# Two build turns per query tile in layer 1, more fill beside the first head, two stores on another queue: a two-layer hybrid block on one core

## The chip, the core and the metric

The kernel runs on one core of a Trainium2 chip. The metric is the device time of one execution in microseconds (us); a time is the median of several executions. TensorE (PE) multiplies matrices into PSUM, VectorE (DVE), ScalarE (ACT) and GpSimd (POOL) work on vectors, and SyncE (SP) issues most transfers. Each engine runs its own instructions in order, and engines wait for one another by semaphores.

## What is computed

Two layers of a block over 1024 tokens and 256 context tokens, width 1024, float32. One projection feeds a gated convolution, a neighbourhood attention (8 heads) and a window attention (8 query heads, 2 key heads); their gated outputs are projected, merged and added to the input. Cut to what matters here:

```
for l in range(2):
    h  = rms_norm(x,   norm_g[l]) * (1 + scale)   + shift
    hc = rms_norm(ctx, norm_g[l]) * (1 + scale_c) + shift_c
    (a_glu, a_gate, nq, nk, nv, n_gate, wq, wk, wv, w_gate, merge) = split(h @ w_in[l])
    o_na = neighbourhood_attention(rms_norm(nq), rms_norm(nk), nv, context keys and values, rpb)
    o_wa = window_attention(rope(rms_norm(wq)), rope(rms_norm(wk)), wv, context ..., sink)
    y = sigmoid(g_a)*conv_branch(...) + sigmoid(g_b)*((o_na*silu(n_gate)) @ w_b) + sigmoid(g_c)*((o_wa*silu(w_gate)) @ w_c)
    x = x + gate * (y @ w_o)
    ctx likewise, in layer 0 only
```

Head size is 64. A query tile is 128 tokens, so a head has 8 query tiles in layer 1 and 10 in layer 0, where the context has queries too.

## The kernel before

A value is kept as a high part rounded to float32r and a low part, the remainder, and products are sums of several matmuls of such parts. In each layer comes first an **attention stage**, then the branches (gates L932, projections L947) and the output pass (L984).

**What sets the order.** PE's instructions run in the order in which the program writes them (L1015, a manual schedule for PE alone). The order on the other engines is chosen at compile time. So whatever PE has to wait for holds up all PE work written behind it.

**The attention stage** (`attention`, L1018) goes through 16 heads, 0 to 7 neighbourhood heads and 8 to 15 window heads. For each query tile it writes: the scores (`sp`, L582 and L584, with the query half `qst` as the loaded weights); some fill; the turn of the probabilities of an earlier tile (`tp`, L614, 4 or 5 transposes, copied by ACT into `pt`, L617, and split by DVE, L618); the softmax weights of this tile; a step of the build of the next head; more fill; and the product with the values of a tile before (`pv`, L625).

**Fill** (class `Fill`) is PE work that needs no attention result: projections of the head groups (`u_ps`, L339), the convolution's inputs (`glu_g`, `glu_v`) and merge gates (`mg_ps`, L714). `pull(ns)` issues pieces until their estimated time reaches `ns`; what is not used in the attention stage comes right after it, where the merge gates run beside the convolution on DVE.

**The build of a head** (`build_head`, L422) loads raw keys and queries, multiplies them by their norms on POOL (`nrm` L439, `nrmq` L465), and turns them in parts: a **turn** is 4 transposes of 128x128 on PE into `t_ps` (L408; 2 for the context keys), then an ACT copy of the high part (`kh` L449, `qst` L472), then a DVE subtraction for the low part (`kl` L450, `qst` L473). The tile `t_ps` comes from a pool of one buffer (`ps_tr`, `bufs=1`), so the transposes of a turn wait until DVE has read the turn before. A neighbourhood head in layer 1 has five turns, three for keys and two for queries. So have the window heads 8 and 12; the other window heads have the two query turns.

The build is a generator. Its first step issues the loads, step k after it normalises part k and turns part k-1, and the last step turns the last part. Tile 0 of the running head takes the first step; from tile 1 on (even heads) or tile 2 on (odd heads) each tile takes one step (L1052). What is left at the head's end runs before the next head. So in layer 1 a five-turn build ends in tile 6 of an even head and in tile 7, the last, of an odd one.

Head 0 has no head before it. Its build runs ahead of the tiles, with a pull of fill after each step (L1034 to L1038), but none after the last turn. The output pass ends with 16 stores of the result, all issued by POOL (L1009).

Of the kernel before, what the change touches and what calls it, by code (L numbers as in the profile page):

```python
# [18 lines left out]
L = 2  # L19
# [21 lines left out]
KC = 8  # L41
# [9 lines left out]
def hybrid_block_kernel(  # L51
# [9 lines left out]
    nc = tc.nc  # L61
# [460 lines left out]
    def wa_build(l, head, st, lc, pb, hs):  # L522
        u, j = 4 + head // 4, head % 4
        yield from build_head(
            l, st, u, pb, j % 2, False, (256, 4) if j == 0 else None, (j * 64, j) if j % 2 == 0 else None, -0.125
        )
        hs.update(kk=st["k"], qt=st["q"])
# [145 lines left out]
    def load_block(src, pw, eng=(nc.gpsimd, nc.gpsimd)):  # L673
        return chunks_of([load_w(src[:, 4 * i:4 * i + 4, :], pw, eng[i]) for i in range(2)])

    def run(gen):
        for _ in gen:
            pass
# [45 lines left out]
    def mm_tile(name):  # L724
        return ps_mm.tile([128, 512], F32, tag="mm", name=name)
# [3 lines left out]
    def s_tile(name):  # L729
        flip[0] ^= 1  # L730
        if flip[0]:
            return ps_s.tile([128, 1024], F32, tag="s", name=name)
        return ps_t.tile([128, 1024], F32, tag="t", name=name)
# [250 lines left out]
    def output_pass(l, gis, y, ysp, pw, xsrc, norms=None, side=iter(())):  # L984

        dst = out if l == L - 1 else x1_d

        def load(f):
            xr = {}
            for gi in gis:  # L990
                o, n = GROUPS[gi]
                xr[gi] = pw.tile([128, 512], F32, tag="t", bufs=3, name="xr")
                nc.sync.dma_start(out=xr[gi][:, 0:n], in_=xsrc[f][:, o:o + n])
            return load_block(wO[l, f], pw, (nc.vector, nc.vector)), xr

        nxt = load(0)
        for f in range(KC):
            w, xr = nxt
            for gi in gis:
                o, n = GROUPS[gi]  # L1000
                ci = 1 if gi == 2 else 0
                ps = s_tile("wo_ps") if (f * len(gis) + gi) % 2 else mm_tile("wo_ps")
                run(product(w, KC, ysp[gi], n, ps))
                if gi == gis[0] and f + 1 < KC:
                    nxt = load(f + 1)
                nc.vector.scalar_tensor_tensor(
                    y[gi][:, f, :], ps[:, 0:n], mods[l][:, 16 + f, ci:ci + 1], xr[gi][:, 0:n], ALU.mult, ALU.add
                )
                nc.gpsimd.dma_start(out=dst[f][:, o:o + n], in_=y[gi][:, f, :])  # L1009
                if norms:  # L1010
                    norms[gi].add(y[gi][:, f, :], f)
            next(side, None)
            next(side, None)
# [4 lines left out]
    def attention(l, st, lc, pb, fill):  # L1018
        need = {0: 0, 2: 1, 4: 2, 6: 3, 8: 4, 12: 5}
        info = [{} for _ in range(16)]  # L1020
        mask_t = pb.tile([128, 896], F32, name="mask_t")
        nc.sync.dma_start(out=mask_t, in_=wa_mask)
        bias_t = [pb.tile([128, 640], F32, name=f"bias{i}") for i in range(2)]
        for bt in bias_t:
            nc.gpsimd.memset(bt[:, 384:640], 0.0)

        def build(i):
            if i in need:
                fill.finish(f"u{need[i]}")
            if i < 8:  # L1030
                return na_build(l, i, st, lc, pb, info[i])
            return wa_build(l, i - 8, st, lc, pb, info[i])

        first = build(0)  # L1034
        next(first)
        fill.pull(FIRST_NS)
        for _ in first:
            fill.pull(1500.0)  # L1038
        last = []
        for i in range(16):  # L1040
            nxt = None
            tiles = na_tiles(l, i, lc, pb, info[i], bias_t, mask_t) if i < 8 else wa_tiles(l, i - 8, st, lc, pb, info[i], mask_t)
            for n, tile_ in enumerate(tiles):
                tile_.scores()
                f = FILL_NS[l] * (0.6 if tile_.w == 0 else 1.0)
                fill.pull(f * 0.5)
                if len(last) > TL - 1:
                    last[-TL].turn()
                tile_.weights()
                if n == 0 and i < 15:  # L1050
                    nxt = build(i + 1)
                if nxt is not None and (n == LOAD_AT or n > BUILD_AT[l][i % 2]):  # L1052
                    next(nxt, None)
                fill.pull(f * 0.5)
                if len(last) > TL:
                    last[-TL - 1].values()
                last = last[-TL:] + [tile_]
            if nxt is not None:
                run(nxt)
        for i in range(TL, 0, -1):  # L1060
            last[-i].turn()
            fill.pull(1800.0)
            last[-i - 1].values()
        fill.pull(1800.0)
        last[-1].values()
        flush()
# [113 lines left out]
    for l in range(L):  # L1180
# [3 lines left out]
        fill = Fill()  # L1184
# [48 lines left out]
        y = {gi: py.tile([128, KC, GROUPS[gi][1]], F32, name=f"y{gi}") for gi in range(ngr)}  # L1233
# [149 lines left out]
```

## Time and profile before

| | us |
|---|---|
| median of three runs | 2761.24 (2760.91 to 2761.47) |
| the profiled execution's own time | 2762.03 |
| its span, first to last instruction | 2759.1 |
| PE busy in the span | 2687.4 (97%) |
| DVE, ACT, POOL busy | 1783.4, 1133.0, 865.9 |

The profile is of one execution; the 2.9 us between its time and its span lie outside the instructions. With one engine busy for 97% of the span, the question for any change is where that engine waits: the rows are read for PE's idle pieces, given in brackets behind the instruction that followed them, with the instruction that ended them. Layer 1's attention stage lies from about 1599 us to 2110 us of the span. The granted clock is the share of TensorE's full speed.

### The profile page before, as it was taken

What the parts mean: (1) busy time and instruction counts of PE and PEld (TensorE: products, weight loads), DVE (VectorE), ACT (ScalarE), POOL (GpSimd) and SP (SyncE); (2) the same over time, 40 slices, a digit from 0 to 9 for tenths busy, and PEclk for the clock granted to TensorE, in tenths of its full rate; (3) what the DMA queues carried; (4) which work ended last, traced back from release to release, by engine and by line L of the source; (5) the groups of instructions that cost most, each with busy time, mean ns of one, the idle gap of its engine ahead of it and who ended that gap; (6) DMA issues with size and microseconds to landing.
All of it is one profiled execution on the core that took longest, in us unless ns stands there. A gap on an engine that the chain in (4) does not pass through costs nothing. (4 is left out here: it accounts for less than half of the span.)

```text
span 2759.1 us, 43655 instructions
## 1 busy us (share of the span) xinstructions
PE 2687.4 (97%) x14996; PEld 2342.2 (85%) x14996; DVE 1783.4 (65%) x3842; ACT 1133.0 (41%) x2500; POOL 865.9 (31%) x1122
## 2 busy tenths in 40 slices
PE   7899999999999999999999999999999999999999
PEld 3899998989888888787888899999888888778887
DVE  4667777766499934778375566766765699372162
ACT  2466666656511113321333356655556322232220
POOL 0044374633400004245501123375424200235610
PEclk9999999999999999999999999999999999999999
DMA  7365444211233332645364355452212243354343
GB/s 253 95 177 151 128 118 117 73 52 35 87 115 115 117 100 73 210 143 177 101 194 157 101 150 155 136 142 86 81 41 78 93 145 111 105 182 139 103 151 105
DMA packets 321293, 337.35 MB, mean 122 GB/s; under 512 B 81840, under 2 KB 240688, under 8 KB 321072
## 3 DMA queue, kind: packets, MB, share of 16 engines
q1 hardware_dynamic: 300848, 296.81, 36.3%
q10 hardware_dynamic: 17280, 28.32, 2.7%
q0 software_dynamic: 2944, 9.44, 0.9%
q8 instruction: 118, 1.93, 0.3%
q14 instruction: 103, 0.84, 0.1%
HBM read 244.02 MB, written 90.44 MB: 121 GB/s over the span
## 5 line engine op out<-in xcount | busy, mean ns | idle before, releaser
L714 PE MATMUL mg_ps<-hh,wf 128*128 128x512 f32 (+1 forms) x1920 | 565.9, 374 | 2.3 <-POOL wf L670 1.3
L339 PE MATMUL u_ps<-wu,hh 128*128 128x384 f32 (+2 forms) x1872 | 485.0, 342 | 9.9 <-DVE vr L371 4.2
L714 PEld LDWEIGHTS mg_ps<-hh,wf 128*128 128x128 f32 x1920 | 347.1, 188 | 69.4 <-POOL wf L670 2.1
L670 POOL TENSOR_TENSOR wf<-rf,wf 128x512 fp32r<-128x512 f32 x118 | 156.6, 1329 | 706.6 <-ACT wf L669 701.0
L714 PE MATMUL mg_ps<-hl,wf 128*128 128x512 f32 (+1 forms) x960 | 356.8, 372 | 0.0
L608 POOL TENSOR_SCALAR p<-p,rd 128x640 f32<-128x640 f32 (+1 forms) x288 | 216.4, 752 | 406.4 <-DVE rd L606 240.5
L339 PEld LDWEIGHTS u_ps<-wu,hh 128*128 128x128 f32 x1872 | 318.8, 190 | 15.4 <-DVE vr L371 4.5
L600 ACT ACTIVATE p<-p,nmx 128x641 f32<-128x641 f32 (+3 forms) x288 | 222.2, 771 | 236.2 <-DVE nmx L596 112.8
L339 PE MATMUL u_ps<-wu,hl 128*128 128x384 f32 (+2 forms) x936 | 312.4, 334 | 0.7 <-DVE hl L274 0.7
L669 ACT ACTIVATE wf<-rf 128x512 fp32r<-128x512 f32 x240 | 150.6, 628 | 342.1 <-PE pp_ps L714 165.5
L714 PE MATMUL pp_ps<-ogh,wf 128*128 128x512 f32 (+1 forms) x960 | 279.6, 373 | 5.0 <-ACT ogh L865 2.4
L714 PE MATMUL gt_ps<-hh,wf 128*128 128x512 f32 (+1 forms) x960 | 284.0, 377 | 0.0
L618 DVE TENSOR_TENSOR pt<-tp,pt 128x640 fp32r<-128x640 f32 (+1 forms) x288 | 215.7, 749 | 98.7 <-ACT pt L617 96.1
L916 ACT ACTIVATE mg_t<-mg_ps 128x512 f32<-128x512 f32 (+1 forms) x120 | 66.6, 555 | 361.2 <-PE mg_ps L714 360.8
L714 PEld LDWEIGHTS pp_ps<-ogh,wf 128*128 128x128 f32 x960 | 174.7, 189 | 42.7 <-ACT ogh L865 3.7
L714 PEld LDWEIGHTS mg_ps<-hl,wf 128*128 128x128 f32 x960 | 180.4, 188 | 33.2
L714 PEld LDWEIGHTS gt_ps<-hh,wf 128*128 128x128 f32 x960 | 174.0, 188 | 36.5 <-issue 1.9
L614 PE MATMUL tp<-ident,p 128*128 128x128 f32 x1280 | 187.4, 273 | 15.6 <-DVE pt L618 7.2
L772 DVE SCALAR_TENSOR_TENSOR cv_out<-cv_in,lc_conv_w,cv_out 128x1024 f32<-128x1024 f32 (+1 forms) x192 | 194.2, 1011 | 0.0
L617 ACT ACTIVATE pt<-tp 128x640 fp32r<-128x640 f32 (+1 forms) x288 | 181.8, 631 | 20.6 <-PE tp L614 19.4
L614 PEld LDWEIGHTS tp<-ident,p 128*128 128x128 f32 x1280 | 153.5, 140 | 43.1 <-POOL p L608 13.8
L714 PE MATMUL wo_ps<-hh,wf 128*128 128x512 f32 (+1 forms) x640 | 184.1, 372 | 0.0
(174 smaller groups left out, 5459.5 us busy)
## 6 DMA issues: line engine op xcount, KB each, us to landing
rf<-in_wF SPq DMA_DIRECT2D x144, 256.0 KB, 2.8
ru<-in_wU SPq DMA_DIRECT2D x104, 192.0 KB, 3.5
bias<-in_na_bias SPq DMA_DIRECT2D x96, 192.0 KB, 2.6
w_ada_s<-in_w_ada SPq DMA_DIRECT2D x64, 256.0 KB, 3.3
nrm<-qk_d SPq DMA_DIRECT2D x40, 320.0 KB, 4.2
rf<-in_wP SPq DMA_DIRECT2D x48, 256.0 KB, 2.7
rf<-in_wO SPq DMA_DIRECT2D x48, 256.0 KB, 3.4
v_d<-vr SPq DMA_DIRECT2D x80, 128.0 KB, 2.0
```

The source lines that it names most:

```text
L339: nc.tensor.matmul(ps[:, c0:UW], lhsT=a[:, k, off * 128:(off + 1) * 128], rhs=w[:, b, c0:UW], start=(k == 0 and i == 0), stop=(k == KC - 1 ...
L600: nc.scalar.activation(self.p[:, 0:n], self.p[:, 0:n], AF.Exp, bias=m, scale=1.0 if sink is None else -1.0, accum_out=self.den)
L608: nc.gpsimd.tensor_scalar(p, p, rd, 1.0, ALU.mult, ALU.mult)
L614: nc.tensor.transpose(tp[:, c * 128:(c + 1) * 128], self.p[:, c * 128:(c + 1) * 128], ident)
L617: nc.scalar.activation(self.pt[:, 0:nch, 0, :], tv, AF.Copy)
L618: nc.vector.tensor_tensor(self.pt[:, 0:nch, 1, :], tv, f32(self.pt[:, 0:nch, 0, :]), ALU.subtract)
L669: nc.scalar.activation(w[:, 0, 0:n, :], raw[:, 0:n, :], AF.Copy)
L670: eng.tensor_tensor(w[:, 1, 0:n, :], raw[:, 0:n, :], f32(w[:, 0, 0:n, :]), ALU.subtract)
L714: nc.tensor.matmul(ps[:, 0:n], lhsT=w(k, b), rhs=a[:, k, 0:n], start=(k == 0 and i == 0), stop=(k == kn - 1 and i == 2),)
L772: nc.vector.scalar_tensor_tensor(r, a[:, k:k + n], tap, r, ALU.mult, ALU.add)
L916: nc.scalar.activation(t[:, 0:n], ps[:, 0:n], AF.Tanh, scale=0.5)
```

## The change

In `attention`, in layer 1 alone, tiles 3 and 5 take a second step of the build. In the build of head 0, in both layers, each pull of fill is of 2300 ns instead of 1500. In the output pass of layer 1 the stores of the last row block (f = 7) are issued by SP instead of POOL; there are two, one for each token group.

```diff
-                nc.gpsimd.dma_start(out=dst[f][:, o:o + n], in_=y[gi][:, f, :])
+                queue = nc.sync if l == L - 1 and f == KC - 1 else nc.gpsimd
+                queue.dma_start(out=dst[f][:, o:o + n], in_=y[gi][:, f, :])
...
         for _ in first:
-            fill.pull(1500.0)
+            fill.pull(2300.0)
...
                 if nxt is not None and (n == LOAD_AT or n > BUILD_AT[l][i % 2]):
                     next(nxt, None)
+                    if l > 0 and n in (3, 5):
+                        next(nxt, None)
```

What this moves on PE is seen at the build of head 2 in layer 1. Before, its last two turns stand in tiles 6 and 7 of head 1, the last one shortly ahead of head 2's first scores (`sp`, the row with `qst_18002`). The names are the program's with buffer numbers; [waits ...] is what the instruction waits for.

```order
L408 MATMUL t_ps_18401<-ident_80,nrmq_18000 128x2x8x8 [waits DVE_49]
L408 MATMUL t_ps_18401<-ident_80,nrmq_18000 128x2x8x8 x3
L339 MATMUL u_ps_18352<-wu_18030,hh0_16251 128x384 x2
L339 MATMUL u_ps_18352<-wu_18030,hl0_16252 128x384
```

That is the turn in tile 6; the one in tile 7, the last on PE before the switch of heads, is this:

```order
L408 MATMUL t_ps_18472<-ident_80,nrmq_18000 128x2x8x8 [waits DVE_49]
L408 MATMUL t_ps_18472<-ident_80,nrmq_18000 128x2x8x8 x3
L339 MATMUL u_ps_18453<-wu_18015,hh1_16871 128x384 x2
L339 MATMUL u_ps_18453<-wu_18015,hl1_16872 128x384
L339 MATMUL u_ps_18453<-wu_18020,hh1_16871 128x384 x2
L339 MATMUL u_ps_18453<-wu_18020,hl1_16872 128x384
L625 MATMUL pv_18486<-pt_18394,vp_18124 128x256 [waits DVE_49]
L625 MATMUL pv_18486<-pt_18394,vp_18176 128x256
L625 MATMUL pv_18486<-pt_18394,vp_18241 128x256 [waits DMAHW7_49]
L625 MATMUL pv_18486<-pt_18394,vc_17492 128x256 x2
L582 MATMUL sp_18497<-kh_17998,qst_18002 128x256 [waits DVE_49]
```

Between the two turns lies a tile's whole work (its own rows are left out here). Now the same two turns on PE stand next to each other in tile 5.

```order
L408 MATMUL t_ps_18375<-ident_80,nrmq_18065 128x2x8x8 [waits DVE_49]
L408 MATMUL t_ps_18375<-ident_80,nrmq_18065 128x2x8x8 x3
L408 MATMUL t_ps_18382<-ident_80,nrmq_18065 128x2x8x8 [waits DVE_49]
L408 MATMUL t_ps_18382<-ident_80,nrmq_18065 128x2x8x8 x3
L339 MATMUL u_ps_18294<-wu_17985,hh0_16251 128x384 x2
L339 MATMUL u_ps_18294<-wu_17985,hl0_16252 128x384
```

The second turn keeps its wait for DVE, and no other matmul stands between the two. Such pairs stand at 16 places of layer 1: one in the build of each of the heads 1, 3, 5, 7, 10 and 14, and two in that of each of the heads 2, 4, 6, 8 and 12. Before there is none.

In layer 1's head 0 the last turn is followed on PE by the scores at once, before:

```order
L339 MATMUL u_ps_17455<-wu_17245,hl1_16872 128x384
L408 MATMUL t_ps_17459<-ident_80,nrmq_17240 128x2x8x8 [waits DVE_49]
L408 MATMUL t_ps_17459<-ident_80,nrmq_17240 128x2x8x8 x3
L582 MATMUL sp_17472<-kh_17238,qst_17242 128x256 [waits DVE_49]
L582 MATMUL sp_17472<-kl_17239,qst_17242 128x256
```

and now:

```order
L339 MATMUL u_ps_17490<-wu_17245,hl1_16872 128x384
L408 MATMUL t_ps_17494<-ident_80,nrmq_17240 128x2x8x8 [waits DVE_49]
L408 MATMUL t_ps_17494<-ident_80,nrmq_17240 128x2x8x8 x3
L582 MATMUL sp_17507<-kh_17238,qst_17242 128x256 [waits DVE_49]
L582 MATMUL sp_17507<-kl_17239,qst_17242 128x256
```

Those four rows stand as they did; what has moved is the fill ahead of the turn (five chunks of the projection now stand between the last two turns, three before).

## Rows read from the trace of the kernel before

**Rows 1.** The page: the span, and PE's line of busy times.
```profile
span 2759.1 us, 43655 instructions
PE 2687.4 (97%) x14996; PEld 2342.2 (85%) x14996; DVE 1783.4 (65%) x3842; ACT 1133.0 (41%) x2500; POOL 865.9 (31%) x1122
```
**Rows 2.** Stretches (length; PE, PEld, DVE, ACT, POOL busy; clock, DMA): layer 0's first build, layer 1's attention.
```profile
138.00:152.00 14.00, 13.92 (x88) 13.13 (x88) 5.38 (x12) 5.78 (x15) 7.27 (x8) 1.00 0.74 212
...
1599.00:2075.00 476.00, 466.57 (x3103) 440.26 (x3103) 324.44 (x897) 280.61 (x674) 212.69 (x327) 1.00 0.39 110
```
**Rows 3.** PE's waits, 1599 to 2075 us (us in total, times, longest).
```profile
PE sp L582 <- DVE qst L473: 4.6, 4, 1.4
PE tp L614 <- DVE rs_a L109: 2.4, 2, 1.3
```
**Rows 4.** Timeline (start, length): the last turn before head 6, to its first scores.
```profile
1812.55 0.60 PE L408 MATMUL t_ps<-ident,nrmq 128*128 128x128 f32 x4
...
1813.81 0.69 ACT L617 ACTIVATE pt<-tp 128x640 fp32r<-128x640 f32 x1
...
1814.40 0.58 ACT L472 ACTIVATE qst<-t_ps 64x512 fp32r<-64x512 f32 x1
...
1815.38 0.68 DVE L473 TENSOR_TENSOR qst<-t_ps,qst 64x512 fp32r<-64x512 f32 x1
...
1816.12 0.39 PE L582 MATMUL sp<-kh,qst 128*128 128x256 f32 x1 [1.34 <-DVE qst L473]
```
**Rows 5.** Timeline: the last turn before head 0 of layer 1, with idle engines.
```profile
1597.03 0.65 PE L408 MATMUL t_ps<-ident,nrmq 128*128 128x128 f32 x4
...
1599.08 0.38 PE L582 MATMUL sp<-kh,qst 128*128 128x256 f32 x1 [1.40 <-DVE qst L473]
```
**Rows 6.** Timeline: the first and the last of 16 turns, PE's part and DVE's.
```profile
1611.72 0.60 PE L408 MATMUL t_ps<-ident,nrm 128*128 128x128 f32 x4
...
1613.67 0.74 DVE L450 SCALAR_TENSOR_TENSOR kl<-t_ps,kg,kh 128x512 fp32r<-128x512 f32 x1
...
2075.75 0.60 PE L408 MATMUL t_ps<-ident,nrmq 128*128 128x128 f32 x4
...
2077.54 0.68 DVE L473 TENSOR_TENSOR qst<-t_ps,qst 64x512 fp32r<-64x512 f32 x1
```
**Rows 7.** Timeline: a turn that waits for the turn before it (layer 0).
```profile
331.54 0.44 PE L408 MATMUL t_ps<-ident,nrmq 128*128 128x128 f32 x2 [0.49 <-DVE qst L473]
```
**Rows 8.** Timeline: three of PE's longer idle pieces.
```profile
73.38 0.62 PE L339 MATMUL u_ps<-wu,hh 128*128 128x384 f32 x2 [2.00 <-ACT hh L273]
...
695.37 0.74 PE L614 MATMUL tp<-ident,p 128*128 128x128 f32 x5 [1.81 <-DVE pt L618]
...
2443.45 0.80 PE L714 MATMUL pp_ps<-ogl,wf 128*128 128x512 f32 x1 [1.71 <-DVE ogl L866]
```
**Rows 9.** Stretches of 2 us behind those pieces (the figure after five engines is the clock).
```profile
74.00:76.00 2.00, 1.57 (x5) 1.58 (x6) 2.00 (x4) 1.19 (x2) 0.00 (x0) 0.65 0.37 98
76.00:78.00 2.00, 2.00 (x8) 2.00 (x8) 1.77 (x3) 1.03 (x2) 0.00 (x0) 0.50 0.00 0
...
696.00:698.00 2.00, 1.42 (x11) 1.21 (x11) 1.27 (x4) 1.56 (x3) 0.87 (x2) 1.00 0.49 173
...
2444.00:2446.00 2.00, 2.00 (x6) 1.57 (x5) 0.71 (x2) 1.15 (x2) 0.58 (x1) 0.50 1.01 380
```
**Rows 10.** Timeline of PE: the last wait of the convolution's norm in layer 1.
```profile
2432.69 1.10 PE L822 MATMUL ln_pr<-ln_s,ones 128*128 128x512 f32 x2 [0.61 <-DVE ln_in L824]
```
**Rows 11.** Timeline at the end of the span: the last result and its store.
```profile
2753.31 0.75 DVE L1006 SCALAR_TENSOR_TENSOR y<-wo_ps,mod,xr 128x512 f32<-128x512 f32 x1 [4.85 <-PE wo_ps L714]
2754.36 0.54 POOL L1009 DMA_DIRECT2D out_y<-y  x1 [5.06 <-DVE y L1006]
```
**Rows 12.** DMA issues: tile, queue, count, KB each, median us from issue to landing.
```profile
out_y<-y POOLq DMA_DIRECT2D x16, 256.0 KB, 3.2
...
act_a_d<-ln_in SPq DMA_DIRECT2D x16, 256.0 KB, 2.5
```

## The prediction, made before the changed kernel was run

> **What bounds the kernel now.** I read the page's busy line first: TensorE (PE) is busy for 2687.4 of 2759.1 us [rows 1]. So a change is worth what it adds to or takes from PE's idle time, and the busy time of the other engines matters only where PE waits for them. The number of PE's instructions and their sizes stay the same here; only their places change.
>
> Then I looked at the stage that the change touches. In 1599 to 2075 us, the attention of layer 1, PE is busy for 466.6 of 476 us [rows 2]; 9.4 us are idle. PE's waits there show which: 4.6 us in four waits of the first scores of a head for the DVE half of the query (`qst`), 2.4 us for small DVE work of a projection, the rest below 1 us each [rows 3]. The four are the target of the first two edits: heads 0, 2, 4 and 6. The largest is head 0's with 1.40 us [rows 5], the next head 6's with 1.34 us [rows 4]. So 3.2 us of the 4.6 belong to the heads 2, 4 and 6.
>
> Why does PE wait there? The timeline of head 6's switch answers it [rows 4]. The last turn's transposes end at 1813.15. ACT is still behind: it copies the probabilities until 1814.50 and then `qst` until 1814.98; DVE follows and ends at 1816.06, and PE's scores start at 1816.12. From the end of the transposes to the end of DVE's read are 2.9 us, and PE had other work for only half of it. I call this time the **latency of a turn**; the whole prediction hangs on it.
>
> **Part 1, the double steps: what they remove.** All builds of layer 1 now end by tile 5, so at each switch DVE is two tiles ahead. I take the 3.2 us of the heads 2, 4 and 6 as gone. One 128 KB load of context values for each neighbourhood head goes out on SP a tile or two earlier; no PE wait in this stage names a load, so I cost it at nothing (if its cover were gone, PE would show a wait for `vc`).
>
> **Part 1, what they add.** The second step of a tile issues a turn directly behind another one, with nothing on PE between, at 16 places (counted in the order shown above). `t_ps` has one buffer, so the second turn has to wait until DVE has read the first. Such a wait exists in the trace: in layer 0 a turn waited 0.49 us for the DVE read of the one before, even with a tile's work between [rows 7]. Queued behind the waiting transposes on PE are the tile's fill, its product with the values, and the next scores; DVE and ACT get nothing new from PE meanwhile. So PE idles for the whole latency of the first turn of each pair.
>
> For the price I went through the 16 turns in the trace of before that become the first of a pair and took for each the end of the transposes and the end of the DVE read. The first of them: 1612.32 to 1614.41, 2.09 us; the last: 2076.35 to 2078.22, 1.87 us [rows 6]. The other 14 lie between 1.76 and 3.33 us; the 16 together are 38.9 us, 2.43 us on average. With 0.05 us from DVE's end to PE's start [rows 4] I get 39.8 us. These latencies hold a part that will stay in a pair, since ACT and DVE must first finish the probabilities' copy of the same tile, which the transposes ahead of the turn released. From below the price is bounded by a turn with idle engines, 1.40 us [rows 5], or 22 us; from above by the longest, 3.3 us, or 53 us. I take the turns' own values, because the same work stands ahead of them on ACT and DVE as before. Below nothing it can't go: PE does nothing new in that time.
>
> **Part 1, the clock.** An idle piece of 2.00 us at 71.4 us was followed by a stretch at a granted clock of 0.50, 1.2 instead of 2.4 GHz; so was one of 1.71 us that had another 0.53 us of idleness shortly before it; one of 1.81 us was not [rows 8, 9]. Behind the first, 0.35 of one stretch of 2 us and 0.50 of the next were withheld [rows 9]: 0.35 x 2 + 0.50 x 2 = 1.7 us of PE work, lost in full where PE is the bound. Of the 16 latencies 13 are over 2.0 us and 3 below 1.9. The bounds are 0 and 13 x 1.7 = 22 us. With one row of about this length each way I expect a fall behind about half of the 13: 7, or 11.9 us.
>
> **Part 2, more fill beside head 0.** In layer 0 the first build has next to no idle time to fill: PE is busy 13.92 of 14 us there [rows 2]. In layer 1 the one wait of note is that of 1.40 us behind the last turn [rows 5], and there the order shows the scores still directly behind the turn: no pull stands between. ACT and DVE are idle ahead of it, so it can't get shorter either. I cost this edit at 0. It takes 6 x 0.8 and 5 x 0.8 us of fill out of what is left for later, which is the cover of the convolution's norm; the norm's last PE wait, 0.61 us [rows 10], then has less ahead of it. I leave up to 2 us for that in the range. Such shifts of the fill could also gain or lose a part of the 2.4 us and smaller waits of the stage [rows 3].
>
> **Part 3, the last stores.** The last DVE result ends at 2754.06, POOL starts to issue at 2754.36 [rows 11], and such a store lands 3.2 us after its issue, against 2.5 us for a transfer of the same size and direction on SP [rows 12]. 0.3 + 0.7 is 1.0 us; SP is at its program's end, so nothing stands behind it. SP picks up a result some 0.1 us after it, so I take 0.9 us. The Trainium skill, page DMA: Bandwidth & Descriptors, section Latency and other measured facts, gives about 0.6 us to the first byte on the hardware path and about 1 us on GpSimd's; by that the gain in landing would be 0.4 us instead of 0.7, an estimate that changes the sum by 0.3 us. The first of the two stores goes out 5.6 us earlier and decides nothing.
>
> **The sum.** The profiled execution took 2762.03 us with a span of 2759.1. Added: 39.8 (pairs) + 11.9 (clock); taken away: 3.2 (switches) + 0.9 (store). That is +47.6 us, or 2809.6 on the profiled execution. The median of the runs is 0.8 us below that execution, so the forecast is 2761.2 + 47.6 = 2808.8, said as 2808.
>
> **The rivals.**
> - *No fall of the clock.* The pairs cost their latency alone: 39.8 - 4.1 = +35.7, 2797. For it: three of the four pieces that I looked at closely were not lone pieces, and 1.81 us alone did nothing. Against: 2.00 us did.
> - *A fall behind nearly every pair.* 39.8 + 22 - 4.1 = +57.7, 2819. For it: every idle piece from 2.0 us that I looked at has one.
> - *Short pairs.* If ACT and DVE, less loaded because PE pauses, read a turn as fast as in [rows 5], the pairs cost 22 to 23 us and no clock: +18.5, 2780. Against: the probabilities' copy of the same tile always stands ahead.
> - *The pairs cost nothing* (the other side). If PE passed the waiting transposes and did fill from behind them, only the gains would be left: -3.2 - 0.9 = -4.1, 2757; with all of the stage's smaller waits gone too, at most -9, 2752. It decides below 4.1 / 16 = 0.26 us a pair. Against it: at 1814.8 PE stood for 1.34 us before the scores although the fill behind them was ready [rows 4]. On this the Trainium skill, page TensorE: Matmul & The Clock Gate, section Step-by-step: what each phase is for, says that PE pulls weight loads ahead while matmuls keep the program's order; the trace agrees with the 1.34 us.
>
> **How the numbers follow.** Forecast 0.50; no fall 0.24; falls nearly everywhere 0.15; short pairs 0.07; nothing 0.04. The predicted time is the forecast's. The range takes in the no-fall case with somewhat shorter pairs (2.0 us each, 2790) and the case of many falls with somewhat longer ones: 2786 to 2824. Left out are the short pairs, the costless ones and some of the high end, near 2 in 10. A measurement of this kernel can tell 0.2% (5.5 us) from no change. Only the last rival can be within 0.2% (0.02, at -4.1 us) or faster by more (0.02, with the smaller waits); all others are slower by 0.5% or more: 0.96.
>
> **What would show it right or wrong.** In the changed kernel: PE's waits list `t_ps` waiting for DVE (`kl` or `qst`) some 16 times, about 2.4 us each, near 39 us in all; the waits of `sp` for `qst` shrink from four to the one of head 0; PE's busy time grows by slowed matmuls, with a granted clock below 1.00 in several stretches between 1610 and 2080; the span from the last DVE result to the end shrinks by about 1 us. The layers' other stages keep their lengths within 2 us. I am wrong if the waits behind the pairs are well under 1.5 us, or if the stage is no longer than before.

## The result, and the profile after

The changed kernel takes 2833.74 us (median of four runs, 2832.97 to 2836.71) beside 2761.35 us of the kernel before in the same comparison: a ratio of 1.026, 95% interval 1.0248 to 1.0273, or +72.4 us. The forecast was +47.6 us; the range ended at 2824. The direction was right, the size was not. The page, answering to [rows 1]:

```profile
span 2834.8 us, 43637 instructions
...
PE 2715.3 (96%) x14996; PEld 2365.3 (83%) x14996; DVE 1786.1 (63%) x3842; ACT 1137.4 (40%) x2500; POOL 867.3 (31%) x1120
```

The span grew by 75.7 us; the profile is of the slowest of the four runs. PE issues the same number of matmuls (PEld is its loading of weights), but is busy 27.9 us longer: that is a slower clock (over all stretches of 2 us to the end of the span, the share of the clock withheld times 2 sums to about 43 us, before to about 13). The other 47.8 us are idle time. PE's waits over the whole span (us in total, times, longest) show where:

```profile
PE t_ps L408 <- DVE kl L450: 22.4, 9, 3.9
PE t_ps L408 <- DVE qst L473: 17.1, 7, 2.7
...
PE mg_ps L714 <- ACT wf L669: 7.7, 2, 3.9
PE pp_ps L714 <- DVE y L976: 6.5, 4, 4.7
...
PE ln_pr L822 <- DVE ln_in L824: 4.5, 3, 1.7
...
PE sp L582 <- DVE qst L473: 1.4, 1, 1.4
```

The first two rows are the pairs: 16 waits, 39.5 us. The last row answers to [rows 3]: of four waits at head switches one is left, head 0's. The three rows between name other work. In the kernel before the same three read 1.0, 1.2 and 1.5 us: 15 us have come in the merge gates and behind the convolution, where the prediction expected nothing. The two waits of `mg_ps` for `wf` are the first merge gate of each layer, 3.74 us in layer 0 and 3.92 us in layer 1.

One pair in the timeline (start, length; in brackets PE's idle time before), answering to [rows 4, 6]:

```profile
1679.39 0.60 PE L408 MATMUL t_ps<-ident,nrmq 128*128 128x128 f32 x4
...
1680.11 0.68 ACT L617 ACTIVATE pt<-tp 128x640 fp32r<-128x640 f32 x1
...
1680.70 0.58 ACT L472 ACTIVATE qst<-t_ps 64x512 fp32r<-64x512 f32 x1
...
1681.69 0.68 DVE L473 TENSOR_TENSOR qst<-t_ps,qst 64x512 fp32r<-64x512 f32 x1
...
1682.43 0.66 PE L408 MATMUL t_ps<-ident,nrmq 128*128 128x128 f32 x4 [2.43 <-DVE qst L473]
```

PE ends the first turn at 1679.99. ACT must first copy the probabilities (`pt`), then the turn's high part; DVE reads last and ends at 1682.37; the second turn starts 0.06 us later. Stretches of 2 us around it, and around another pair at 1631 (length; PE, PEld, DVE, ACT, POOL busy; clock, DMA share, GB/s), answering to [rows 9]:

```profile
1680.00:1682.00 2.00, 0.00 (x0) 0.00 (x0) 1.30 (x3) 1.27 (x4) 1.40 (x2) 1.00 0.53 125
1682.00:1684.00 2.00, 1.57 (x10) 1.58 (x11) 0.63 (x2) 0.88 (x3) 2.00 (x3) 0.90 0.05 18
1684.00:1686.00 2.00, 2.00 (x9) 2.00 (x8) 1.04 (x3) 0.47 (x3) 0.00 (x0) 0.50 0.20 66
1686.00:1688.00 2.00, 2.00 (x12) 2.00 (x11) 0.50 (x1) 0.00 (x0) 0.00 (x0) 0.74 0.31 98
...
1632.00:1634.00 2.00, 1.22 (x8) 1.22 (x9) 0.96 (x3) 0.47 (x1) 0.00 (x0) 1.00 0.01 2
1634.00:1636.00 2.00, 2.00 (x15) 2.00 (x14) 0.80 (x2) 0.00 (x0) 0.00 (x0) 1.00 0.00 0
```

Behind the 2.43 us the clock was withheld by 0.10, 0.50 and 0.26 of three stretches: (0.10 + 0.50 + 0.26) x 2 = 1.7 us of PE work. I call such a place a **fall** of the clock. Behind the 2.15 us at 1631 there was none. Going through all stretches of layer 1's attention in this way, 11 of the 16 pairs have a fall: 1.7 us each, 3.4 behind the longest, 20.5 us together.

By stages, the difference to the kernel before (the ends of stages are PE's first instruction of a kind; the last two columns are the experiments with the double steps alone and with the fill alone, told below):

| stage | before, us | changed | steps alone | fill alone |
|---|---|---|---|---|
| start to layer 1's first projection | 1530.90 | +12.9 | -0.2 | +17.4 |
| to the first branch gate of layer 1 | 853.94 | +65.7 | +57.1 | +5.0 |
| to the last output product | 368.43 | -1.4 | -1.0 | -2.0 |
| to the end of the span | 5.8 | -1.4 | 0.0 | +0.4 |

The first stage holds no double step. So layer 0 alone lost 12.9 us, to the edit that the prediction had costed at nothing.

### The profile page after: what moved, and what is told of

Its sections match the earlier page's. It is cut to its first block, busy times and chain, and to the rows that moved or that the text cites. A ratio compares the mean times of both kernels' runs of the same rounds, so it can differ in the third digit from the quotient of the medians.

```text
span 2834.8 us, 43637 instructions
## 1 busy us (share of the span) xinstructions
PE 2715.3 (96%) x14996; PEld 2365.3 (83%) x14996; DVE 1786.1 (63%) x3842; ACT 1137.4 (40%) x2500; POOL 867.3 (31%) x1120
## 3 DMA queue, kind: packets, MB, share of 16 engines
q8 instruction: 118, 1.93, 0.3%
## 4 chain that ended last, share of the span: by engine, by line
PE 79%; DVE 8%; ACT 4%; DMA 3%; issue 3%; POOL 2%; SPq 0%; DVEq 0%; POOLq 0%; ACTq 0%
PE mg_ps L714 21%; PE u_ps L339 14%; PE pp_ps L714 8%; PE gt_ps L714 8%; PE wo_ps L714 7%; PE pv L625 4%; PE tp L614 4%; PE glu_v L714 3%; PE glu_g L714 3%; PE sp L582 2%; PE sp L584 2%; PE t_ps L408 1%; DVE pt L618 1%; DVE p L591 1%; ACT p L600 1%
## 5 line engine op out<-in xcount | busy, mean ns | idle before, releaser
L339 PE MATMUL u_ps<-wu,hh 128*128 128x384 f32 (+2 forms) x1872 | 492.1, 346 | 12.2 <-DVE vr L371 4.2
L339 PEld LDWEIGHTS u_ps<-wu,hh 128*128 128x128 f32 x1872 | 325.3, 194 | 17.8 <-DVE vr L371 4.5
L714 PEld LDWEIGHTS pp_ps<-ogh,wf 128*128 128x128 f32 x960 | 175.1, 189 | 47.8 <-DVE y L976 9.0
```

Of the source, the lines that this page charges most:

```text
L339: nc.tensor.matmul(ps[:, c0:UW], lhsT=a[:, k, off * 128:(off + 1) * 128], rhs=w[:, b, c0:UW], start=(k == 0 and i == 0), stop=(k == KC - 1 ...
L714: nc.tensor.matmul(ps[:, 0:n], lhsT=w(k, b), rhs=a[:, k, 0:n], start=(k == 0 and i == 0), stop=(k == kn - 1 and i == 2),)
```

## The parts apart

Each comparison below has its own runs of the kernel before; their medians lie between 2758.77 and 2762.84 us, and differences are taken within a comparison.

**The double steps alone** (`e1_steps`).

```diff
                     next(nxt, None)
+                    if l > 0 and n in (3, 5):
+                        next(nxt, None)
```

> Only the double steps of layer 1 (tiles 3 and 5), without the other two edits. The changed kernel's trace has 16 waits of a turn for the turn before, 39.5 us in all, and some 20 us of withheld clock in layer 1's attention. Theory A (the pairs and the clock falls behind them make nearly all of the loss of that stage): +39.5 - 3.2 + about 20 = +56 us, 2817. My prediction's own terms (7 falls): +48.5, 2810. Rival B (the loss in layer 1 needs the shifted fill too): clearly less, +35 us or below.

Measured 2819.85 us against 2762.84, a ratio of 1.0209 (1.0194 to 1.0225), +57.0 us. Its waits in layer 1's attention:

```profile
PE t_ps L408 <- DVE kl L450: 21.9, 9, 3.0
PE t_ps L408 <- DVE qst L473: 18.0, 7, 3.0
```

39.9 us, nearly as in the changed kernel. The rest is clock: the stage from head 0's scores to the first merge gate is 55.6 us longer, of which 17.4 are busy time. Of the 12 pairs that waited 2.30 us or longer nine have a fall here, and a pair of 1.93 us, some 1.2 us behind another wait of 1.68, has a double one: (9 + 2) x 1.7 = 18.7 us.

**The fill alone** (`e2_fill`).

```diff
-            fill.pull(1500.0)
+            fill.pull(2300.0)
```

> Only the larger pulls of fill beside head 0, 2300 ns instead of 1500, in both layers. My prediction: 0 us (up to 2). Theory A (the first merge gate and the end of the convolution's norm now wait longer, and the clock falls behind both): in the changed kernel layer 1's projections begin 12.9 us later, and the first merge gate of layer 1 waits 3.9 instead of about 2.7 us with a fall behind it: +13 to +18 us, 2774 to 2779. Rival B (layer 0's loss is made by something else, such as the order on the other engines): within 3 us of the kernel before.

Measured 2782.01 us, 1.0067 (1.0053 to 1.0081), +19.2 us.

**The stores alone** (`e3_stores`), the change's third part without the others.

> Only the last two stores on SP. Prediction: -0.9 us (0.4 to 1.5), 2760.4. Rival: the end of the program does not depend on which engine issues the last store, 0 us.

Measured 2762.29 us over 11 runs, 0.9997 (0.9989 to 1.0006): -0.5 us, which the runs can't tell from nothing. The trace can: SP picks up the last result (DVE's end at 2755.33) at once,

```profile
2754.58 0.75 DVE L1006 SCALAR_TENSOR_TENSOR y<-wo_ps,mod,xr 128x512 f32<-128x512 f32 x1 [4.85 <-PE wo_ps L714]
...
2755.36 0.34 SPq L1010 DMA_DIRECT2D out_y<-y  x1
```

and the span ends about 3.5 us after that issue, at 2758.8; in [rows 11] POOL issues 0.30 us after DVE's end and the span ends about 4.7 us later. From PE's last matmul to the end it is 5.8 us before and 4.3 us here. In all 16 traces of this study the figure lies between 5.8 and 6.2 us with the stores on POOL and at 4.3 or 4.4 us with them on SP. The last store's own landing has little part in it: it comes 2.3 us after the issue on POOL and 2.0 us after it on SP. About 1 us of the gain lies between the landing and the end of the span (2.4 us on POOL, 1.4 on SP); what fills that time no run here shows.

The three alone add up to 57.0 + 19.2 - 0.5 = 75.7 us; together they cost 72.4. So the parts hardly touch one another, and the miss is to be looked for in each.

## What a pair costs: the buffer, the cover and the clock

**One piece of fill between the two turns** (`e5_one`), the double steps otherwise alone.

```diff
+                    if l > 0 and n in (3, 5):
+                        for _ in range(1):
+                            if fill.items:
+                                fill.step()
+                        next(nxt, None)
```

> The double steps alone, with one piece of fill (about 1 us of TensorE work) between the two turns; fill of layer 0 and stores as before. Theory A (latency minus cover, and a fall of the clock behind only the longest idle pieces): 16 waits of t_ps shrink from 2.4 to about 2.0 us for those that are split, near 32 us in all, 6 falls of 1.7 us = 10 us, minus 3.2 us at the head switches: about +39 us over before, 2800. Rival C (the clock's loss follows the idle time in proportion, 20.5 us for 39.5 us of waits, whatever the length of a piece): +45 us, 2806. Rival D (one piece in front is enough to restart ACT and DVE, so that the pair costs only what is left of 2.4 us after a piece with a long matmul): waits under 1 us each, +12 us, 2773.

**Three pieces between them** (`e6_three`): the same with `range(3)`.

> The double steps alone, with three pieces of fill between the two turns. Theory A: waits near 1.0 us each, 16 to 17 us in all, hardly a fall of the clock (0 to 2, up to 3.4 us), minus 3.2 us at the head switches: +13 to +17 us, about 2777. Rival C (clock loss in proportion to the idle time): +22 us, 2784. If covered turns cost nothing: -3 us, 2759.

Measured: one piece 2800.47 us, 1.0150 (1.0135 to 1.0165), +41.3; three pieces 2775.79 us, 1.0061 (1.0045 to 1.0078), +16.6, both against 2759.17. The waits of `t_ps`, first with one piece, then with three:

```profile
PE t_ps L408 <- DVE kl L450: 16.8, 9, 2.5
PE t_ps L408 <- DVE qst L473: 14.4, 7, 2.5
```

```profile
PE t_ps L408 <- DVE kl L450: 7.2, 7, 1.4
PE t_ps L408 <- DVE qst L473: 5.1, 6, 1.5
```

39.9, 31.2 and 12.3 us in all. The second pair of head 2 shows what a piece does, without fill, with one piece and with three:

```profile
1669.37 0.66 PE L408 MATMUL t_ps<-ident,nrmq 128*128 128x128 f32 x4 [3.04 <-DVE qst L473]
...
1668.14 0.75 PE L408 MATMUL t_ps<-ident,nrmq 128*128 128x128 f32 x4 [2.53 <-DVE qst L473]
...
1663.44 0.66 PE L408 MATMUL t_ps<-ident,nrmq 128*128 128x128 f32 x4 [1.48 <-DVE qst L473]
```

The first turn's transposes end at 1666.33, 1665.09 and 1660.39 in the three traces, so the second turn starts 3.04, 3.05 and 3.05 us after them. A piece is shorter than the about 1 us that the expectation gave it: here 0.52 us of matmuls, three pieces 1.56 (a piece of the convolution's inputs is 0.70). Each wait is shorter by just that; the latency stands as it was and only its **cover**, the PE work that runs meanwhile, grows. One piece does not restart anything (theory D falls). With one piece eight clock falls follow pairs, 13.6 us; a loss in proportion to the idle time would be 31.2 x 20.5 / 39.5 = 16.2, so this run alone can't tell theory C from A. With three pieces the waits are 1.5 us or shorter, and no fall follows a pair (the stage's one fall stands at its end, at the first merge gate), where C wants 12.3 x 20.5 / 39.5 = 6.4 us. So C falls: what the clock takes depends on single pieces, not on the sum.

**The second turn in another buffer** (`e11_twobuf`). The order of work is that of the double steps; the second turn of a tile writes into the pool that the fill uses (`ps_mm`, two buffers).

```diff
+        if spare[0]:
+            ps = ps_mm.tile([128, 512], F32, tag="mm", name="t_ps")
+        else:
+            ps = ps_tr.tile([128, 512], F32, tag="tr", name="t_ps")
...
+                    if l > 0 and n in (3, 5):
+                        spare[0] = True
+                        next(nxt, None)
+                        spare[0] = False
```

> The double steps alone, with the same order of work, but the second turn of a tile writes its transposes into a buffer of the pool that the fill uses (two buffers) instead of the one buffer of the turns. Theory A (the one buffer of t_ps is what costs): the waits of t_ps for DVE fall from 39.5 us to under 8 us, with some new waits of u_ps or mg_ps for that buffer, under 8 us; no fall of the clock in the stage: 0 to +13 us over before, 2760 to 2773, and about 45 us less than the double steps with one buffer. Rival G (what costs is the latency of ACT and DVE for two turns in a row, whoever holds the buffer): the waits move to tp, u_ps or sp in about the same size, +45 to +57 us, 2805 to 2817.

Measured 2775.80 us, 1.0056 (1.0042 to 1.0070), +17.0 us against 2758.77: 40 us less than with one buffer. PE's longest waits in layer 1's attention:

```profile
PE u_ps L339 <- DVE kl L455: 3.8, 2, 2.0
PE pv L630 <- DVE cb_b L643: 3.7, 1, 3.7
PE tp L619 <- DVE pt L623: 3.0, 2, 1.7
PE u_ps L339 <- DVE vr L371: 2.2, 2, 1.4
PE t_ps L413 <- DVE vr L371: 1.8, 2, 1.1
```

No `t_ps` waits for a turn any more; the fill (`u_ps`) and `t_ps` wait for each other's buffer at six places, 7.8 us in all. Rival G falls: ACT and DVE keep up with two turns in a row, it is the one buffer that stopped PE. By the median it costs 4 us more than theory A allowed; the profiled execution, 2770.84 us, is the fastest of the four and 12.1 us above before, inside A's span. Its rows show two parts. One is that sharing. The other is the wait of `pv` for `cb_b`, with the stage's one fall behind it: it is 2.7 us with the double steps alone and 2.8 us with one piece of fill, 0.7 us in the whole kernel before, and stands where the neighbourhood heads end. Why the double steps make it I have not settled, and what the slower three executions spent more is not shown.

## What the larger pulls cost

**Layer 0 alone** (`e7_fill0`).

```diff
-            fill.pull(1500.0)
+            fill.pull(2300.0 if l == 0 else 1500.0)
```

> 2300 ns instead of 1500 ns a pull in the first build of layer 0 alone; layer 1 and everything else as before. Theory A (the fill spent early in layer 0 is missing as cover of the merge gates and of the convolution's norm there; layer 1 gives only its own wait in front of the merge gates): +13 to +18 us, 2774 to 2779. Rival E (the two layers share the loss of 19 us about evenly): +8 to +11 us, 2769 to 2772.

Measured 2774.16 us, 1.0052 (1.0037 to 1.0067), +15.0 us against 2759.17: most of the edit's 19.2 comes from layer 0. In layer 1 PE waits 3.97 us in one piece at the first merge gate with the fill alone, where before three waits make 2.7 us together, and the clock has a double fall of 3.4 us there. Two places of layer 0 show the rest. The first, in the changed kernel, is the first merge gate:

```profile
689.97 0.45 SPq L656 DMA_DIRECT2D act_c_d<-ob  x1
690.52 6.78 SPq L667 DMA_DIRECT2D rf<-in_wF  x4
...
693.71 1.39 ACT L669 ACTIVATE wf<-rf 128x512 fp32r<-128x512 f32 x2 [1.36 <-DMA rf<-in_wF]
...
694.39 0.79 PE L714 MATMUL mg_ps<-hh,wf 128*128 128x512 f32 x1 [3.74 <-ACT wf L669]
```

The load of the gate's weights (`rf`) goes out behind a store of attention results on SP's queue, 0.14 us before PE has nothing else to do, so PE stands for its whole way: landing, ACT's rounding, 3.74 us in one piece. The clock answers as behind a pair, but with a double fall, 3.4 us with the two stretches after these:

```profile
692.00:694.00 2.00, 0.00 (x0) 0.00 (x0) 0.71 (x4) 0.64 (x3) 0.80 (x1) 0.94 0.75 250
694.00:696.00 2.00, 1.46 (x3) 0.74 (x4) 0.00 (x0) 0.97 (x2) 1.58 (x2) 0.50 0.00 1
696.00:698.00 2.00, 2.00 (x8) 1.90 (x9) 0.00 (x0) 0.28 (x1) 0.94 (x1) 0.50 0.40 136
```

In the kernel before the load went out at 694.21, during a turn's wait of 1.81 us [rows 8], and PE still had attention work until 697.18; the gate then waited 0.58 us and soon after 0.63, and no stretch there has a clock below 1.00. So in idle time this place lost little, 3.74 us in one piece against 1.81 + 0.58 + 0.63 = 3.02 us in three; most of its loss is the clock's 3.4 us. The second place is behind the attention. The stretches from the last product with values to the first branch gate, and from there to the last one, of the kernel before, then of this run:

```profile
749.37:1055.40 306.03, 306.03 (x1576) 258.07 (x1575) 230.01 (x322) 60.14 (x110) 3.76 (x4) 1.00 0.34 112
1055.40:1361.52 306.12, 300.40 (x1571) 250.84 (x1570) 206.88 (x384) 78.52 (x147) 147.11 (x129) 1.00 0.47 144
```

```profile
761.68:1062.12 300.44, 300.44 (x1552) 253.53 (x1551) 230.23 (x322) 59.59 (x109) 3.82 (x4) 1.00 0.34 111
1062.12:1376.16 314.04, 303.37 (x1571) 252.78 (x1570) 208.05 (x384) 79.16 (x147) 145.87 (x129) 0.99 0.46 140
```

The first stretch is merge gates, the cover of the convolution, and it is 5.6 us shorter: what the first build took early is missing here. The second stretch, in which PE waits for the convolution's norm and what follows from it, is 7.9 us longer, with a piece of 4.34 us and a fall of the clock. From the first turn to the last branch gate layer 0 grew by 13.2 us: 5.3 up to the first branch gate, where the first merge gate's wait lies, and 7.9 behind it. In the nine traces of this study whose layer 0 is that of before, this length lies between 1219.8 and 1223.9 us, so 13.2 us are far outside the scatter of single executions, and differences of 2 us are not.

**Both places mended** (`e13_end`): the larger pulls in layer 0, and the time set aside for that load doubled. So some tiles run without fill before the first merge gate, and as much gate work is left for later.

```diff
-END_NS = 4000.0
+END_NS = 8000.0
```

> The larger pulls in layer 0's first build alone (which gave +15 us), and the time set aside for the load of the first merge weights, when the fill passes from projections to merge gates, raised from 4000 to 8000 ns of fill: some two more tiles pass before the first merge gate, and about 4 us of gates stay for the stretch behind the attention. Theory A (the loss in layer 0 is the wait of the first merge gate with its slower clock, and 5.6 us of gates that are missing beside the convolution): mg_ps no longer waits (4.1 us before), some of it comes back as waits of tp in the two tiles (2 to 4 us), and the waits behind the convolution shrink: +5 to +9 us over before, 2764 to 2768. Rival H (the loss is due to the attention of layer 0 running with shifted fill, not to these two places): +13 to +17 us as without it.

Measured 2762.39 us over 10 runs, 1.0011 (1.0001 to 1.0020), +2.5 us against 2759.88, less than theory A's +5 to +9. The same two stretches:

```profile
749.67:1054.31 304.64, 304.64 (x1570) 256.93 (x1569) 230.04 (x322) 60.05 (x110) 3.76 (x4) 1.00 0.33 112
1054.31:1359.25 304.94, 299.60 (x1571) 251.02 (x1570) 205.55 (x384) 79.05 (x147) 146.36 (x129) 1.00 0.47 144
```

The gate no longer waits (PE's waits around it are 0.8 and 0.9 us, for the attention), 4.2 of the 5.6 us of cover are back, and of layer 0's 13.2 us nothing is left: from the first turn to the last branch gate it is 1.7 us shorter than before the change, which is within the scatter. Rival H falls. `END_NS` holds in both layers, and layer 1 pays for it: its branch gates take 237.27 us instead of 234.88, with a wait of 3.41 us for `ogh` and a double fall where before stood the 1.71 us of [rows 8] and a single one. The edit moves both causes at once, so their separate sizes, 5.3 and 7.9 us, rest on the lengths of the stages, not on a run of each.

**The convolution's pace** (`e8_fillshare`, `e14_endshare`): `SHARE[0]`, the share of the time of the gates behind the attention that the convolution's work on DVE is allowed, from 0.8 to 0.9; once with the larger pulls in both layers, once on top of `e13_end`. The expectations of `e8_fillshare` and of `e12_share` further down call it layer 0's; it holds in both layers.

> 2300 ns a pull in both layers, as in the run of the fill alone (+19 us), and in layer 0 the share of the convolution's pacing raised from 0.8 to 0.9, so that the convolution is done earlier beside the attention. Theory A (the loss comes where the convolution's norm and the gates behind it lost their cover): in layer 0 the waits of pp_ps and ln_pr near 1115 to 1155 us and the clock's fall behind them shrink, the merge gates' wait near 692 us stays: +8 to +13 us, 2770 to 2775. Rival F (the loss has nothing to do with the convolution's place): the same +19 us, 2781; slower still, if the faster convolution takes DVE from the attention.

> As e13_end, with the share of the convolution's pacing (which holds in both layers, beside the gates behind the attention) raised from 0.8 to 0.9. Theory A: nothing of layer 0's loss is left but the moved waits of the attention, and layer 1 gains 4 to 5 us as in e12_share: -4 to +2 us, 2755 to 2761. Rival H: +6 us or more, 2765 and above.

Measured 2772.26 us, 1.0045 (1.0030 to 1.0060), +13.1 us, where the larger pulls alone gave +19.2; and 2758.71 us, 0.9995 (0.9986 to 1.0005), -1.2 us. In the first, layer 0's second stretch is 303.52 us instead of 315.37 with the pulls alone, while the wait of the first merge gate stays, 4.4 us. The stretch of merge gates ahead of it is 3.0 us longer, so 8.8 us net. So most of the part behind the convolution can be had back by starting its work earlier, as theory A says, whose span ends at +13. In the second, rival H's +6 us and more falls. Its trace does not bear out all of theory A: layer 0 is 3.3 us longer there than before, with a wait of 2.90 us behind the convolution and two falls, and layer 1's branch gates are 6.8 us shorter.

## Other ways to the same aim

**The build one tile earlier** (`e4_early`), no double steps, stores on SP.

```diff
-BUILD_AT = ((0, 1), (0, 1))
+BUILD_AT = ((0, 1), (0, 0))
```

> The gain without the price: in layer 1 odd heads begin their build's steps in tile 1 like even ones, one step a tile, so that no two turns stand together and every build ends in tile 6; with the stores on SP. Theory A (the waits of the heads 2, 4 and 6 were the lateness of the last turn): -3.2 - 0.9 = -4.1 us, 2757.2. Rival B (the earlier steps wait for their loads, or another wait takes the place): 0 or slower by 1 to 5 us.

Measured 2770.79 us, 1.0030 (1.0019 to 1.0041), +8 us: rival B's way, and more than its 5 us. The waits at the switches of heads 2, 4 and 6 went, and others came:

```profile
PE t_ps L408 <- DMA ru<-in_wU: 4.8, 1, 4.8
PE t_ps L408 <- POOL nrm L439: 4.5, 2, 3.0
```

The second row names what isn't there yet one tile earlier: POOL's norm of the raw keys. The turn waits on PE, and all fill behind it. The first row names a load that the turn doesn't read, but the weight load of the same turn names POOL's norm too, which ends at 1646.65:

```profile
1645.61 1.04 POOL L439 TENSOR_TENSOR nrm<-nrm,rstd 128x512 f32<-128x512 f32 x1
...
1646.70 0.72 PEld L408 LDWEIGHTS t_ps<-ident,nrm 128*128 128x128 f32 x4 [5.01 <-POOL nrm L439]
```

So both rows are one cause. At the two longest of these waits, 4.8 and 3.0 us, the clock had a fall each.

**Only the last turn moved** (`e9_last`), stores on SP. In layer 1 the step of tile 7 stands right behind that tile's scores, with a whole tile's fill between it and the next head.

```diff
                 tile_.scores()
+                if l > 0 and n == 7 and nxt is not None:
+                    next(nxt, None)
```

> An edit in place of the double steps: in layer 1 the build step of tile 7 is taken right behind that tile's scores, ahead of the fill, instead of behind the tile's softmax weights, so that a last turn has a whole tile's fill between it and the next head's scores; no two turns stand together. The two last stores on SyncE's queue as in the change. Fill as before. Theory A: the three waits of sp for qst at heads 2, 4 and 6 (3.2 us together) go, nothing is added: -3 to -4 us, 2758. Rival B (the early turn of tile 7 waits for POOL's norm or for t_ps, or shifts ACT's and DVE's work so that tp waits instead): 0 to +4 us, 2762 to 2766.

Measured 2754.94 us over 11 runs, 0.9980 (0.9971 to 0.9989), -5.0 us against 2759.90, where theory A said -3 to -4; the stores' 1.5 us of the traces and the 3.2 us of the switches make 4.7. The turn now starts ahead of the transposes of the probabilities, so ACT takes its copy at once:

```profile
1806.42 0.58 ACT L472 ACTIVATE qst<-t_ps 64x512 fp32r<-64x512 f32 x1
...
1807.03 0.69 DVE L473 TENSOR_TENSOR qst<-t_ps,qst 64x512 fp32r<-64x512 f32 x1 [0.17 <-ACT qst L472]
1807.21 0.71 PE L614 MATMUL tp<-ident,p 128*128 128x128 f32 x5
```

The three waits of 3.2 us at heads 2, 4 and 6 are gone; the only one of `sp` for `qst` is head 0's 1.4 us. This is what the double steps were after, without a pair.

**Head 0's wait as well** (`e10_cover`): the same, and layer 1's first build has its fill in six smaller pulls, the sixth behind the last turn.

```diff
-            fill.pull(1500.0)
+            fill.pull(1500.0 if l == 0 else 1250.0)
+        if l > 0:
+            fill.pull(1250.0)
```

> As e9_last, and in layer 1's first build the same 7500 ns of fill as before the change is spread over six pulls of 1250 ns instead of five of 1500 ns, the sixth behind the last turn, where head 0's scores waited 1.40 us. Theory A: that wait goes too, about 1.3 us less than e9_last: -4 to -5 us, 2757. Rival B: the same total of fill moves the waits among the turns before it, no gain over e9_last.

Measured 2755.20 us over 11 runs, 0.9983 (0.9974 to 0.9993): no gain over `e9_last`. Head 0's wait is gone from the list, but `t_ps` waits 2.0 us in four places there instead of 1.0 in two, and `tp` for `rs_a` 2.1 instead of 1.1 us: the wait moved.

**With the convolution's pace** (`e12_share`): `e9_last` and `SHARE[0]` of 0.9.

> As e9_last (step of tile 7 ahead of the fill, two stores on SyncE's queue, fill as before), with the share of the convolution's pacing in layer 0 raised from 0.8 to 0.9. Theory A (the convolution's norm lacks cover even with the old fill: 5 us of waits between 1108 and 1252 us in before): 1 to 4 us less than e9_last, 2751 to 2754. Rival F (the waits only move from the norm into the attention of layer 0, where DVE gets more to do): the same as e9_last, 2755, or up to 3 us more.

Measured 2748.97 us, 0.9964 (0.9951 to 0.9978), -9.8 us against 2758.77: the fastest of this study, below both kernels and 2 us under theory A's span. Against `e9_last` layer 0 is 1.6 us shorter from its first turn to its last branch gate, which is within the scatter, and layer 1's stretch of branch gates 6.1 us; there the wait of 1.71 us of [rows 8] and the fall of the clock behind it are gone. So the gain came in layer 1 and not, as theory A had it, in layer 0. With the larger pulls the same pace had won 9.7 us in layer 0: most of that was the cover that the pulls had taken.

## Why the prediction was wrong, and where it was right

The measured +72.4 us lie above the range, which ended at +63. The step that failed most is "I cost this edit at 0", the larger pulls; the fall of the clock behind "about half of the 13" was too small as well. The double steps and the stores alone, 57.0 - 0.5 = 56.5 us, would have stayed inside the range.

- **The pairs: right.** 39.8 us forecast (its terms, 38.9 + 16 x 0.05, make 39.7), 39.5 in the changed kernel and 39.9 alone, at 16 places. Reading each turn's latency in the trace of before, from the end of PE's transposes to the end of DVE's read, gave the price, since the same copy of the probabilities stands ahead on ACT. The sum is closer than its parts: single waits differ from their forecast by up to 1.2 us, both ways, and that this cancels is luck in part. `e11_twobuf` shows the cause: with a second buffer 40 of the 57 us are gone. The rivals of short pairs and of costless pairs are out.
- **The head switches: right.** 3.2 us less was forecast; the waits of `sp` for `qst` went from 4.6 to 1.4 us, as said.
- **The clock: mechanism right, term too small.** The step that failed is the fall behind "about half of the 13", 7, or 11.9 us. In the changed kernel it was 11 of the 13 pairs that waited over 2.0 us, 20.5 us, or 8.6 us more; with the double steps alone 18.7 us. The choice rested on one row each way, and the row without a fall, 1.81 us, was shorter than nearly all of the pairs to be priced. What the prediction kept as the rival of "a fall behind nearly every pair", +57.7 us, is what the double steps did: +57.0 alone.
- **The fill: wrong.** "I cost this edit at 0" failed: +19.2 us alone. The prediction saw the right object, the cover of the convolution's norm, but priced it by the wait that happens to be left in layer 1, 0.61 us [rows 10], and allowed 2 us. What is left with the cover there doesn't say what appears once it is thinner: in layer 0 5.6 us less of it gave 7.9 us. And it looked for cover only behind the convolution. That fill also sets when the merge gates begin, and so whether their first weights are there (the 3.74 us in one piece, with a double fall behind it), was not in the sum; the same came in layer 1 (3.92 us). So "the layers' other stages keep their lengths within 2 us" was wrong for layer 0, by 12.9 us.
- **The stores: the way right, the size too small.** -0.9 us forecast; 1.5 us in the traces: about 0.3 us of pick-up and 1.2 us between issue and end, where the medians of [rows 12] had given 0.7. Those are medians over 16 transfers each, and the last store is not like them: its landing gained only 0.2 to 0.3 us, and about 1 us came behind the landing, which was not in the sum. The estimate that the prediction made from the Trainium skill (DMA: Bandwidth & Descriptors, Latency and other measured facts), 0.4 us for the landing, is nearer to that than the 0.7 of the rows. The times of the runs can't show a gain of this size.

The miss is 72.4 - 47.6 = 24.8 us: the fill's 19.2 (its clock falls among them), the clock behind the pairs 8.6, the stores -0.6 are 27.2; the 2.4 us left are within what the separate runs leave open.

## What to carry to other kernels

Two uses of a single-buffered tile written next to each other on an in-order engine cost the whole way through its readers, each time; read that way off the trace, then see whether another buffer, or moving one use ahead of other work, has the same effect for less. Work used as filler is also cover for whatever stands behind it: before it is spent earlier, find what starts when it ends, which loads are issued there, and how long that stretch must be. Where PE is the bound, price most of the new idle pieces that are as long as those followed by slowed matmuls elsewhere in the trace with a fall of its own: here 11 and 9 of the 12 longest pairs had one, not half.

## What was not expected of the hardware

- The clock's falls came in steps of 1.7 us of withheld work. In the changed kernel 11 of the 12 pairs that waited 2.30 us or longer had one and none of the 4 that waited 2.15 us or less; with the double steps alone it was 9 of such 12, and one of 1.93 us that stood shortly behind another wait; with one piece of fill between, waits of 1.87 and 2.03 us had one and one of 2.26 us had none. With waits up to 1.5 us none followed a pair. So the length of one piece orders the cases but doesn't decide them; what else does is open.
- The last store landed 2.3 us after its issue on POOL's queue and 2.0 us on SP's, but the span ended 4.7 and 3.5 us after that issue: most of the difference between the queues stands behind the landing. Its cause is open.
